# One scatter for both experts of a pair, slots turned back behind the second product, and nine load buffers

## The chip, the cores and the metric

The kernel runs on one core of one Trainium2 chip. The time is the device time of one execution, in microseconds (us). The core has TensorE for matmuls, VectorE (DVE) and ScalarE (ACT) for element by element work, GpSimd (POOL, hardly used here) and SyncE (SP), whose queue issues the loads. Each engine runs its instructions in the order in which they were laid down when the program was built, and waits on semaphores for the others.

## The reference, cut to what matters

The program is a two-layer hybrid transformer block on 256 tokens (and 256 context tokens in the first layer) of width 1024. Only the last part matters here, the mixture of experts of the second layer:

```python
def swiglu(h, w1, w3, w2):
    return (jax.nn.silu(h @ w1) * (h @ w3)) @ w2

def moe_swiglu(h, w_router, w1, w3, w2):
    logits = jnp.einsum('bnd,de->bne', h, w_router).astype(jnp.float32)
    top_vals, top_idx = lax.top_k(logits, TOP_K)          # 2 of 8 experts
    gates = jax.nn.softmax(top_vals, axis=-1)
    combine = jnp.einsum('bnk,bnke->bne', gates, jax.nn.one_hot(top_idx, N_EXPERTS, dtype=jnp.float32))
    out = jnp.zeros_like(h)
    for e in range(N_EXPERTS):
        out = out + combine[..., e:e + 1].astype(h.dtype) * swiglu(h, w1[e], w3[e], w2[e])
    return out
...
        x_lat = x_lat + mod_lat[5] * y
```

All is fp32. `w1` and `w3` are 1024 x 3584 for each expert, `w2` 3584 x 1024.

## The kernel before, in words

Experts are sorted by the number of their tokens and taken in pairs: the even expert of a pair has up to 128 slots, the odd one up to 64. A token is brought to its slot by a product with a one-hot matrix (`hot`, L1331), and the expert's rows go back by a product with the one-hots turned (`pT`).

An expert's inner width of 3584 is cut into 7 blocks of 512. `seq` (L172) gives the order of the blocks: those of a pair's two experts take turns (the first pair starts with two blocks of the even one). For each block, `experts` (L1428) does the first product with `w1` and `w3` (`hidden`, into the banks `p1` and `p3`), then the second product of the block before with `w2` (`finish`, into two banks `py` that gather all 7 blocks), so the second product runs one block late. `turn` puts the hidden values through SiLU and transposes them; TensorE's transposes stand inside the next block's first product, and ScalarE and VectorE then make `g` (odd expert) or `gh` and `gl` (even expert), which the second product needs.

Weights come in loads of 1 MiB (`load`, L106) into `raw` buffers that are used in a ring: 4 + 1 + 5 = 10. An fp32 product is done as two or three products of rounded parts, so ScalarE casts each load (`whi`, L76) and VectorE subtracts (`wlo`, L77), here called the cast and the split. There are four buffers of such pairs. A load may start when the split ten places back is done. A block takes six loads.

Once a pair, in the fourth block of the even expert, `slots_back` (L1381) transposes the pair's one-hots, copies them to `pT` (ScalarE), multiplies them with the gates and copies the result to `gs` (VectorE): the gate of each slot. One block later `one_hots` overwrites `hot` for the next pair. When an expert's 7 blocks are done, `rows` (L1515) scales its result by the gates and rounds it in two parts, `yh` (ScalarE) and `yl` (VectorE). In the next block `scatter` (L1524) multiplies them with `pT`, between the products with `w1` and `w3`, and `residual` (L406) adds eight pieces of 128 x 256 to the tokens `xl` on VectorE (L409). So each expert of a pair has its own scatter, except in the last pair, where `scatter_last` takes both. A second pass over all experts stands behind a branch and does not run here.

The order on each engine is laid down by a scheduler, which starts from the order of the code; `tc.issue_after` holds an instruction back behind another. The names in the rows: `whi`, `wlo` the parts of weights, `p` the first product, `py` the second, `pt` transposes, `pg` gates or gathered tokens, `po` the scatter's product, `u`, `g`, `sl`, `gl` steps of `turn` and of the hidden values, `xf`, `xs` gathered tokens.

Of the kernel before, what the change touches and what calls it, by code (L numbers as in the profile page):

```python
# [20 lines left out]
P = 128  # L21
# [9 lines left out]
EPS = 1e-6  # L31
RAW, RAW0, RAWF, RAW2, RAW3, WS, WS2 = 4, 5, 3, 5, 1, 3, 4
TURN = (3, 5)
# [14 lines left out]
def program(ctx, tc, a, out, upto=99, tap=None):  # L48
# [6 lines left out]
    def pool(name, bufs=1, **kw):  # L55
        return tc.tile_pool(name=name, bufs=bufs, **kw)
# [11 lines left out]
    def bank(name="ps"):  # L68
        return ps.tile([P, 512], F32, tag="ps", name=name)
# [32 lines left out]
    def buffers(*pools):  # L102

        ring[:] = [p for p, n in pools for _ in range(n)]
# [72 lines left out]
    def small_(e):  # L177
        return e % 2 == 1
# [1082 lines left out]
    wsp_st.close()  # L1261
    if RAW3:
        raw3 = ctx.enter_context(pool("raw3", RAW3, reuse_waits="tile"))
        buffers((rawp, RAW), (raw3, RAW3), (raw2, RAW2))
    wsw = ctx.enter_context(pool("wsw", WS2, reuse_waits="tile"))
# [114 lines left out]

    def slots_back(p2):  # L1381
        pt = bank("pt")
        for i in range(4):
            TE.transpose(pt[:, P * i:P * (i + 1)], hot[:, i % 2, i // 2].bitcast(F32), ident)
        S.copy(pT, pt.rearrange("p (e t) -> p e t", e=2))
        pg = bank("pg")
        for e in range(2):
            for tt in range(2):
                TE.matmul(pg[:, e:e + 1], hot[:, tt, e].bitcast(F32), gate[:, tt, 2 * p2 + e:2 * p2 + e + 1],
                          start=tt == 0, stop=tt == 1)  # L1390
        V.tensor_copy(gs[:, 2 * p2:2 * p2 + 2], pg[:, 0:2])
# [36 lines left out]
    def experts(x0, then=None):  # L1428
# [86 lines left out]
        def rows(e):  # L1515
            ys = []
            for n in range(2):
                yh, yl = (t512(f"y{z}").bitcast(F32R) for z in "hl")
                S.mul(yh, py[e][n], gs[:, e:e + 1])
                V.scalar_tensor_tensor(yl, py[e][n], gs[:, e:e + 1], yh.bitcast(F32), op0=ALU.mult, op1=ALU.subtract)  # L1520
                ys.append((yh, yl))
            return ys

        def scatter(e, ys):  # L1524
            for d2 in range(KT // 2):
                po = bank("po")
                for z, dt in enumerate((2 * d2, 2 * d2 + 1)):
                    yh, yl = ys[dt // 4]
                    c = slice(P * (dt % 4), P * (dt % 4 + 1))
                    o = po[:, NC * z:NC * (z + 1)]  # L1530
                    TE.matmul(o, yh[:, c], pT[:, e % 2], start=z == 0, stop=False, skip_group_check=True)
                    TE.matmul(o, yl[:, c], pT[:, e % 2], start=False, stop=z == 1, skip_group_check=True)
                for z in range(2):
                    residual(1, 5, 2 * d2 + z, po[:, NC * z:NC * (z + 1)], None, (1,))
# [19 lines left out]
        xg[0] = x0  # L1554
        prev = done = None
        for i, (e, f) in enumerate(seq):
# [6 lines left out]
            if i == 2 and not ids:  # L1563
                for j in range(1, EXP):
                    k = HP * (j % 2) + j // 2
                    ids[j] = nc.values_load(ords[0:1, k:k + 1].bitcast(I32), engines=[mybir.EngineType.SP],
                                            min_val=0, max_val=EXP - 1)
            if done:
                scatter(*done)
                done = None  # L1570
            hidden(p3, e)
# [18 lines left out]
            if i:  # L1590
                finish(i - 1)
                if seq[i - 1][1] == NF - 1:
                    done = seq[i - 1][0], rows(seq[i - 1][0])
            if f == 3 and e % 2 == 0:
                slots_back(e // 2)
            if f == 4 and e < EXP - 2:
                one_hots(e + 2)
        m = finish(len(seq) - 1)
        scatter_last((done, (EXP - 1, rows(EXP - 1))), m)

# [104 lines left out]
```

## Time and profile before

| | |
|---|---|
| time, median of 3 runs | 1754.49 us (1753.9 to 1755.68) |
| the profiled execution | 1755.12 us |
| its span, first to last instruction | 1752.5 us |
| TensorE busy over the span | 1666.5 us (95%) |
| VectorE busy over the span | 1464.7 us (84%) |
| ScalarE busy over the span | 1061.3 us (61%) |
| mixture-of-experts stage | about 848 to 1746 us of the span |
| loads of its weights | 335 of 1 MiB, two halves of a last one |

Times in the rows count from the span's start. Matmuls are pipelined and their ends are modelled, so a busy TensorE is not one at its peak: the distance of the starts tells its pace. Where an instruction waited, the row ends with the idle time of its engine and who ended it.

### The profile page before, as it was taken

The page shows a single profiled execution, that of the slowest core. Times are in us where ns is not written, and L with a number is a line of the kernel's source. Part 1 is how long each engine was busy: PE and PEld are TensorE (multiplying, and loading weights), DVE is VectorE, ACT ScalarE, POOL GpSimd, SP SyncE. Part 2 cuts the span into 40 slices and gives each one's busy share as a digit, 9 for nine tenths or more (in the row PEclk, how much of TensorE's full clock was granted, in tenths as well). Part 3 has the DMA queues.
Part 4 walks back from the last instruction along what each step waited for, and adds up shares of the span by engine and source line. Part 5 has one row for each costly group of instructions (what it writes and reads, how often), then busy time and mean ns, then how long its engine had stood idle before and what let it go on. Part 6 is the DMA issues. An engine that isn't in the chain of part 4 may idle for free.

```text
span 1752.5 us, 23262 instructions
## 1 busy us (share of the span) xinstructions
PE 1666.5 (95%) x8672; PEld 1389.6 (79%) x8672; DVE 1464.7 (84%) x2081; ACT 1061.3 (61%) x1145; POOL 7.4 (0%) x10
## 2 busy tenths in 40 slices
PE   6999999999999999996999989999999999999996
PEld 4777878888888999996877867778877788777885
DVE  5567599978544888886889999999999999999996
ACT  3354342222222455554788878878887788888884
POOL 0000000000000000000000000000000000000000
PEclk9999999999999999997999999999999999999998
DMA  8542554665312121254799999999989999899991
GB/s 363 203 168 107 231 216 168 263 235 198 121 48 96 66 93 66 70 213 144 291 384 386 416 342 343 409 400 412 416 327 389 404 400 419 332 378 420 399 418 65
DMA packets 65930, 474.08 MB, mean 271 GB/s; under 512 B 7312, under 2 KB 7696, under 8 KB 8464
## 3 DMA queue, kind: packets, MB, share of 16 engines
q1 hardware_dynamic: 65376, 471.79, 69.0%
q8 instruction: 70, 1.15, 0.3%
q10 hardware_dynamic: 432, 0.72, 0.1%
q14 instruction: 52, 0.43, 0.1%
HBM read 471.43 MB, written 1.05 MB: 270 GB/s over the span
## 4 chain that ended last, share of the span: by engine, by line
PE 79%; DVE 12%; issue 6%; ACT 2%; DMA 1%; DVEq 0%; SPq 0%; ACTq 0%
PE p L1445 9%; PE py L1511 7%; DVE wlo L77 7%; PE py L1507 5%; PE p L81 5%; PE p L82 5%; PE p L80 5%; PE p L1455 4%; PE p L1456 4%; PE p L1454 4%; PE po L80 3%; PE po L81 3%; PE po L82 3%; PE pp L950 2%; PE pp L949 2%
## 5 line engine op out<-in xcount | busy, mean ns | idle before, releaser
L76 ACT CAST whi<-raw 128x2048 fp32r<-128x2048 f32 (+1 forms) x458 | 760.8, 1683 | 387.1 <-PE p L81 157.4
L77 DVE TENSOR_TENSOR wlo<-raw,whi 128x2048 fp32r<-128x2048 f32 (+1 forms) x458 | 903.0, 2000 | 102.1 <-ACT whi L76 98.4
L1445 PE MATMUL p<-wlo,xs 128*128 128x512 f32 x448 | 176.6, 394 | 8.3 <-DVE wlo L77 8.3
L1445 PE MATMUL p<-whi,xs 128*128 128x512 f32 x448 | 177.8, 397 | 2.4 <-DVE xl L409 2.3
L1455 PE MATMUL p<-wlo,xh 128*128 128x512 f32 x448 | 176.0, 393 | 2.3 <-DVE wlo L77 2.3
L1454 PE MATMUL p<-whi,xh 128*128 128x512 f32 x448 | 177.8, 397 | 0.0
L1456 PE MATMUL p<-whi,xl 128*128 128x512 f32 x448 | 175.8, 392 | 0.0
L81 PE MATMUL p<-hlo,whi 128*128 128x512 f32 (+1 forms) x368 | 139.7, 381 | 0.2
L82 PE MATMUL p<-hhi,wlo 128*128 128x512 f32 (+1 forms) x368 | 139.3, 380 | 0.0
L80 PE MATMUL p<-hhi,whi 128*128 128x512 f32 (+1 forms) x368 | 138.3, 381 | 1.1 <-ACT hhi L372 1.1
L1507 PE MATMUL py<-whi,g 128*128 128x512 f32 x224 | 95.8, 430 | 18.4 <-DVE g L77 18.2
L1445 PEld LDWEIGHTS p<-wlo,xs 128*128 128x128 f32 x448 | 84.2, 188 | 29.7 <-DVE wlo L77 12.9
L1455 PEld LDWEIGHTS p<-wlo,xh 128*128 128x128 f32 x448 | 85.1, 190 | 19.4 <-DVE wlo L77 2.6
L1445 PEld LDWEIGHTS p<-whi,xs 128*128 128x128 f32 x448 | 84.2, 188 | 19.3 <-issue 2.5
L1456 PEld LDWEIGHTS p<-whi,xl 128*128 128x128 f32 x448 | 84.8, 189 | 17.8
L1454 PEld LDWEIGHTS p<-whi,xh 128*128 128x128 f32 x448 | 84.9, 189 | 16.7
L1507 PE MATMUL py<-wlo,g 128*128 128x512 f32 x224 | 93.7, 421 | 0.0
L1511 PE MATMUL py<-wlo,gh 128*128 128x512 f32 x224 | 86.6, 401 | 6.1 <-DVE wlo L77 6.1
L1511 PE MATMUL py<-whi,gl 128*128 128x512 f32 x224 | 87.1, 403 | 0.0
L950 PE MATMUL pp<-wlo,hhi 128*128 128x256 f32 x288 | 81.8, 284 | 1.2 <-DVE wlo L77 1.2
L949 PE MATMUL pp<-whi,hhi 128*128 128x256 f32 x288 | 82.5, 287 | 0.0
L1511 PE MATMUL py<-whi,gh 128*128 128x512 f32 x224 | 82.0, 395 | 0.0
(375 smaller groups left out, 3082.8 us busy)
## 6 DMA issues: line engine op xcount, KB each, us to landing
raw<-moe_w SPq DMA_DIRECT2D x335, 1024.0 KB, 8.2
raw<-ffn SPq DMA_DIRECT2D x33, 1024.0 KB, 4.8
raw<-w_mod SPq DMA_DIRECT2D x24, 1024.0 KB, 7.0
raw<-w_mod_t SPq DMA_DIRECT2D x24, 1024.0 KB, 4.8
raw<-w_in_odd SPq DMA_DIRECT2D x12, 1024.0 KB, 4.7
raw<-w_in_even SPq DMA_DIRECT2D x6, 1024.0 KB, 6.6
raw<-w_out_even SPq DMA_DIRECT2D x4, 1024.0 KB, 7.1
raw<-w_out_odd SPq DMA_DIRECT2D x4, 1024.0 KB, 4.7
```

What stands on the lines that cost most here:

```text
L76: h = S.copy(hi, full)
L77: return h, (eng or V).tensor_tensor(lo, full, hi.bitcast(F32), op=ALU.subtract)
L80: TE.matmul(o, wh, xh, start=first, stop=False, **kw)
L81: TE.matmul(o, wh, xl, start=False, stop=False, **kw)
L82: TE.matmul(o, wl, xh, start=False, stop=last, **kw)
L949: TE.matmul(po, hhi[:, kt, tk], wh[:, c], start=f, stop=False, **kw)
L1445: m = TE.matmul(po, x_, z[:, w], start=kt == 0 and z is wh, stop=kt == KT - 1 and z is wl, skip_group_check=True)
L1454: TE.matmul(po, xh[:, kt], wh[:, w], start=kt == 0, stop=False)
L1455: TE.matmul(po, xh[:, kt], wl[:, w], start=False, stop=False)
L1456: m = TE.matmul(po, xl[:, kt], wh[:, w], start=False, stop=kt == KT - 1)
L1507: m = TE.matmul(py[e][n], gT[:, ft].rearrange("p u s -> p (u s)"), w[:, 512 * n:512 * (n + 1)], start=first and w is wh, stop=last and w i ...
L1511: m = TE.matmul(py[e][n], gT[g][:, ft], w[:, 512 * n:512 * (n + 1)], start=first and g == "h" and w is wh, stop=last and g == "l")
```

## The change

`slots_back` takes the last matmul of the second product (`m`, from `finish`) and puts its transposes and gate matmuls behind it. `rows` gives the even expert tiles of its own (`ep`), so that they can wait; `done` collects both experts of a pair, and one `scatter` adds their four products in the same bank and updates the tokens once: 8 updates a pair instead of 16. For the memory the one-buffer pool `raw3` goes: nine loads in the ring.

```diff
--- before.py
+++ after.py
@@ -29,7 +29,7 @@
 EDIM = 3584
 NF = EDIM // 512
 EPS = 1e-6
-RAW, RAW0, RAWF, RAW2, RAW3, WS, WS2 = 4, 5, 3, 5, 1, 3, 4
+RAW, RAW0, RAWF, RAW2, WS, WS2 = 4, 5, 3, 5, 3, 4
 TURN = (3, 5)
 FK = 7
 KY = (2, 6)
@@ -1259,9 +1259,7 @@
 
 
     wsp_st.close()
-    if RAW3:
-        raw3 = ctx.enter_context(pool("raw3", RAW3, reuse_waits="tile"))
-        buffers((rawp, RAW), (raw3, RAW3), (raw2, RAW2))
+    buffers((rawp, RAW), (raw2, RAW2))
     wsw = ctx.enter_context(pool("wsw", WS2, reuse_waits="tile"))
     pairs[:] = [wsw] * WS2
     W.ahead = 2 * WS2 - 2
@@ -1378,16 +1376,17 @@
 
     gs = mo.tile([P, 2 * EXP], F32, name="gs")[:, :EXP]
 
-    def slots_back(p2):
+    def slots_back(p2, m):
         pt = bank("pt")
-        for i in range(4):
-            TE.transpose(pt[:, P * i:P * (i + 1)], hot[:, i % 2, i // 2].bitcast(F32), ident)
+        pg = bank("pg")
+        with tc.issue_after(m.ins):
+            for i in range(4):
+                TE.transpose(pt[:, P * i:P * (i + 1)], hot[:, i % 2, i // 2].bitcast(F32), ident)
+            for e in range(2):
+                for tt in range(2):
+                    TE.matmul(pg[:, e:e + 1], hot[:, tt, e].bitcast(F32), gate[:, tt, 2 * p2 + e:2 * p2 + e + 1],
+                              start=tt == 0, stop=tt == 1)
         S.copy(pT, pt.rearrange("p (e t) -> p e t", e=2))
-        pg = bank("pg")
-        for e in range(2):
-            for tt in range(2):
-                TE.matmul(pg[:, e:e + 1], hot[:, tt, e].bitcast(F32), gate[:, tt, 2 * p2 + e:2 * p2 + e + 1],
-                          start=tt == 0, stop=tt == 1)
         V.tensor_copy(gs[:, 2 * p2:2 * p2 + 2], pg[:, 0:2])
 
     ep = ctx.enter_context(pool("exp"))
@@ -1515,21 +1514,25 @@
         def rows(e):
             ys = []
             for n in range(2):
-                yh, yl = (t512(f"y{z}").bitcast(F32R) for z in "hl")
+                if small_(e):
+                    yh, yl = (t512(f"y{z}").bitcast(F32R) for z in "hl")
+                else:
+
+                    yh, yl = (ep.tile([P, 512], F32R, tag=f"y{z}{n}", name=f"y{z}") for z in "hl")
                 S.mul(yh, py[e][n], gs[:, e:e + 1])
                 V.scalar_tensor_tensor(yl, py[e][n], gs[:, e:e + 1], yh.bitcast(F32), op0=ALU.mult, op1=ALU.subtract)
                 ys.append((yh, yl))
             return ys
 
-        def scatter(e, ys):
+        def scatter(both):
             for d2 in range(KT // 2):
                 po = bank("po")
-                for z, dt in enumerate((2 * d2, 2 * d2 + 1)):
-                    yh, yl = ys[dt // 4]
-                    c = slice(P * (dt % 4), P * (dt % 4 + 1))
-                    o = po[:, NC * z:NC * (z + 1)]
-                    TE.matmul(o, yh[:, c], pT[:, e % 2], start=z == 0, stop=False, skip_group_check=True)
-                    TE.matmul(o, yl[:, c], pT[:, e % 2], start=False, stop=z == 1, skip_group_check=True)
+                for j, (e, ys) in enumerate(both):
+                    for z, dt in enumerate((2 * d2, 2 * d2 + 1)):
+                        c = slice(P * (dt % 4), P * (dt % 4 + 1))
+                        for k, y in enumerate(ys[dt // 4]):
+                            TE.matmul(po[:, NC * z:NC * (z + 1)], y[:, c], pT[:, e % 2], start=j == z == k == 0,
+                                      stop=j == z == k == 1, skip_group_check=True)
                 for z in range(2):
                     residual(1, 5, 2 * d2 + z, po[:, NC * z:NC * (z + 1)], None, (1,))
 
@@ -1552,7 +1555,7 @@
                             out[:, NC * (dt - 1):NC * (dt + 1)], xs[1][:, dt - 1:dt + 1].rearrange("p k t -> p (k t)"))
 
         xg[0] = x0
-        prev = done = None
+        prev, done = None, []
         for i, (e, f) in enumerate(seq):
             p1, p3 = bank("p1"), bank("p3")
             hidden(p1, e, None if prev is None else lambda m: turn(i - 1, prev, m))
@@ -1565,9 +1568,9 @@
                     k = HP * (j % 2) + j // 2
                     ids[j] = nc.values_load(ords[0:1, k:k + 1].bitcast(I32), engines=[mybir.EngineType.SP],
                                             min_val=0, max_val=EXP - 1)
-            if done:
-                scatter(*done)
-                done = None
+            if len(done) == 2:
+                scatter(done)
+                done = []
             hidden(p3, e)
             if small_(e):
                 prev = [t512("c") for _ in range(2)]
@@ -1588,15 +1591,15 @@
             if i == len(seq) - 1:
                 turn(i, prev)
             if i:
-                finish(i - 1)
+                m = finish(i - 1)
                 if seq[i - 1][1] == NF - 1:
-                    done = seq[i - 1][0], rows(seq[i - 1][0])
+                    done.append((seq[i - 1][0], rows(seq[i - 1][0])))
             if f == 3 and e % 2 == 0:
-                slots_back(e // 2)
+                slots_back(e // 2, m)
             if f == 4 and e < EXP - 2:
                 one_hots(e + 2)
         m = finish(len(seq) - 1)
-        scatter_last((done, (EXP - 1, rows(EXP - 1))), m)
+        scatter_last((*done, (EXP - 1, rows(EXP - 1))), m)
 
     experts(gather(0, True), gates)
     most = nc.values_load(most_i[0:1, 0:1], min_val=0, max_val=NC)
```

The order of the instructions as it was laid down, at three places, all on VectorE. First, pair 1 around `slots_back`, in the seventh block of the pair. Before:

```order
L1474 TENSOR_TENSOR u<-pt,u 128x256 x2
L77 TENSOR_TENSOR wlo<-raw,whi 128x2048
L1476 TENSOR_TENSOR u<-u 128x256
L1391 COPY gs<-pg 128x2
L1338 TENSOR_SCALAR hot<-const 128x128 x3
L77 TENSOR_TENSOR wlo<-raw,whi 128x2048
L77 TENSOR_TENSOR g<-u,g 128x4x64
L1338 TENSOR_SCALAR hot<-const 128x128
L77 TENSOR_TENSOR wlo<-raw,whi 128x2048
L1581 TENSOR_TENSOR sl<-sl,p_10268 128x512
L77 TENSOR_TENSOR wlo<-raw,whi 128x2048 x4
```

After the change:

```order
L1473 TENSOR_TENSOR u<-pt,u 128x256 x2
L77 TENSOR_TENSOR wlo<-raw,whi 128x2048
L1475 TENSOR_TENSOR u<-u 128x256
L77 TENSOR_TENSOR wlo<-raw,whi 128x2048
L77 TENSOR_TENSOR g<-u,g 128x4x64
L77 TENSOR_TENSOR wlo<-raw,whi 128x2048
L1584 TENSOR_TENSOR sl<-sl,p_10253 128x512
L77 TENSOR_TENSOR wlo<-raw,whi 128x2048
L1336 TENSOR_SCALAR hot<-const 128x128
L1390 COPY gs<-pg 128x2
L1336 TENSOR_SCALAR hot<-const 128x128 x3
L77 TENSOR_TENSOR wlo<-raw,whi 128x2048 x3
```

The copy to gs and the one-hots moved from ahead of g to behind sl and a third split. On TensorE the four transposes and the gate matmuls moved from ahead of the sixteen matmuls py<-g to behind them. The first pair had this order before, too.

Second, the end of pair 1, where the next pair's first blocks have begun. In both fences u and g belong to the odd expert's last block, and yl is the odd expert's, whose second product needs g. Before:

```order
L1474 TENSOR_TENSOR u<-pt,u 128x256 x2
L77 TENSOR_TENSOR wlo<-raw,whi 128x2048
L1476 TENSOR_TENSOR u<-u 128x256
L409 SCALAR_TENSOR_TENSOR xl<-po,mods_91,xl 128x256 x2
L77 TENSOR_TENSOR g<-u,g 128x4x64
L409 SCALAR_TENSOR_TENSOR xl<-po,mods_91,xl 128x256 x6
L77 TENSOR_TENSOR wlo<-raw,whi 128x2048 x2
L1581 TENSOR_TENSOR sl<-sl,p_11317 128x512
L77 TENSOR_TENSOR wlo<-raw,whi 128x2048 x2
L1520 SCALAR_TENSOR_TENSOR yl<-py,gs,yh 128x512 x2
L77 TENSOR_TENSOR wlo<-raw,whi 128x2048 x2
L1493 TENSOR_TENSOR gl<-pt,gh 128x512
```

After the change:

```order
L1473 TENSOR_TENSOR u<-pt,u 128x256 x2
L77 TENSOR_TENSOR wlo<-raw,whi 128x2048
L1475 TENSOR_TENSOR u<-u 128x256
L77 TENSOR_TENSOR wlo<-raw,whi 128x2048
L77 TENSOR_TENSOR g<-u,g 128x4x64
L77 TENSOR_TENSOR wlo<-raw,whi 128x2048
L1584 TENSOR_TENSOR sl<-sl,p_11302 128x512
L77 TENSOR_TENSOR wlo<-raw,whi 128x2048
L1523 SCALAR_TENSOR_TENSOR yl<-py,gs,yh 128x512
L77 TENSOR_TENSOR wlo<-raw,whi 128x2048
L1523 SCALAR_TENSOR_TENSOR yl<-py,gs,yh 128x512
L409 SCALAR_TENSOR_TENSOR xl<-po,mods_91,xl 128x256
```

The even expert's eight updates (xl) are gone from both sides of g, and g stands behind two splits here where one stood (four and three, counted from the last xf). Behind these rows come, before, the odd expert's eight updates in a row; after the change, a split, two updates, a split, gl and five updates, each for both experts.

Third, pair 0, where the even expert ends two blocks ahead of the odd one; the place is behind the even expert's second yl. Before:

```order
L77 TENSOR_TENSOR wlo<-raw,whi 128x2048
L409 SCALAR_TENSOR_TENSOR xl<-po,mods_91,xl 128x256 x2
L77 TENSOR_TENSOR wlo<-raw,whi 128x2048
L409 SCALAR_TENSOR_TENSOR xl<-po,mods_91,xl 128x256 x2
L77 TENSOR_TENSOR wlo<-raw,whi 128x2048
L1474 TENSOR_TENSOR u<-pt,u 128x256 x2
L409 SCALAR_TENSOR_TENSOR xl<-po,mods_91,xl 128x256
L1476 TENSOR_TENSOR u<-u 128x256
L409 SCALAR_TENSOR_TENSOR xl<-po,mods_91,xl 128x256 x2
L77 TENSOR_TENSOR g<-u,g 128x4x64
L409 SCALAR_TENSOR_TENSOR xl<-po,mods_91,xl 128x256
L77 TENSOR_TENSOR wlo<-raw,whi 128x2048 x6
```

After the change:

```order
L77 TENSOR_TENSOR wlo<-raw,whi 128x2048 x3
L1473 TENSOR_TENSOR u<-pt,u 128x256 x2
L77 TENSOR_TENSOR wlo<-raw,whi 128x2048
L1475 TENSOR_TENSOR u<-u 128x256
L77 TENSOR_TENSOR wlo<-raw,whi 128x2048
L77 TENSOR_TENSOR g<-u,g 128x4x64
L77 TENSOR_TENSOR wlo<-raw,whi 128x2048 x4
```

The eight updates are gone, and five splits instead of three stand ahead of g.

## Rows read from the trace of the kernel before

**Rows 1.** Busy us by window: total, PE, PEld, DVE, ACT, POOL, clock, DMA share, GB/s
```profile
848.00:1746.00 898.00, 857.58 (x4009) 701.35 (x4007) 845.25 (x623) 723.43 (x609) 0.00 (x0) 0.98 0.94 373
...
1110.00:1160.00 50.00, 49.92 (x229) 40.35 (x228) 49.77 (x31) 43.21 (x35) 0.00 (x0) 1.00 1.01 420
```

**Rows 2.** Chain of waits, 1100 to 1300: start us, us, what
```profile
1105.35 3.94 PE py L1507 x16
...
1134.61 3.92 PE py L1507 x16
...
1168.41 5.43 PE py L1507 x16
...
1198.78 3.63 PE py L1507 x16
...
1256.52 1.75 PE pg L1411 x16
```

**Rows 3.** Table of waits, 800 to 1753: total us, times, longest
```profile
DVE gs L1391 <- PE pg L1389: 11.3, 3, 3.8
...
DVE wlo L77 <- DMA raw<-moe_w: 1.4, 1, 1.4
```

**Rows 4.** Timeline of VectorE, 1150 to 1175: start, us, instruction [idle before <-releaser]
```profile
1165.07 0.16 DVE L1391 COPY gs<-pg 128x2 f32<-128x2 f32 x1 [3.78 <-PE pg L1389]
```

**Rows 5.** Timeline of TensorE, same place
```profile
1163.65 0.60 PE L1384 MATMUL pt<-const,hot 128*128 128x128 f32 x4
1164.09 0.95 PE L1389 MATMUL pg<-const,hot 128*128 128x1 f32 x8
1168.41 0.79 PE L1507 MATMUL py<-whi,g 128*128 128x512 f32 x1 [3.37 <-DVE g L77]
```

**Rows 6.** Timeline of VectorE, end of pair 1
```profile
1293.35 0.41 DVE L77 TENSOR_TENSOR g<-u,g 128x256 fp32r<-128x256 f32 x1
1293.68 2.44 DVE L409 SCALAR_TENSOR_TENSOR xl<-po,mods,xl 128x256 f32<-128x256 f32 x6
```

**Rows 7.** Timeline of ScalarE, end of pair 1
```profile
1299.61 0.69 ACT L1519 ACTIVATE yh<-py,gs 128x512 fp32r<-128x512 f32 x1 [1.59 <-PE py L1507]
```

**Rows 8.** Timeline of TensorE, end of pair 1
```profile
1287.70 0.28 PE L1531 MATMUL po<-pT,yh 128*128 128x256 f32 x1
...
1290.41 0.40 PE L1454 MATMUL p<-whi,xh 128*128 128x512 f32 x1
...
1317.23 0.50 PE L1511 MATMUL py<-wlo,gh 128*128 128x512 f32 x1 [2.09 <-DVE wlo L77]
```

**Rows 9.** Timeline of VectorE, pair 0
```profile
1025.58 0.88 DVE L409 SCALAR_TENSOR_TENSOR xl<-po,mods,xl 128x256 f32<-128x256 f32 x2 [0.47 <-PE po L1532]
...
1033.73 0.41 DVE L77 TENSOR_TENSOR g<-u,g 128x256 fp32r<-128x256 f32 x1
...
1034.46 13.29 DVE L77 TENSOR_TENSOR wlo<-raw,whi 128x2048 fp32r<-128x2048 f32 x6
...
1053.63 0.42 DVE L77 TENSOR_TENSOR g<-u,g 128x256 fp32r<-128x256 f32 x1
```

**Rows 10.** Timeline of TensorE, pair 0
```profile
1029.59 0.47 PE L1445 MATMUL p<-whi,xs 128*128 128x512 f32 x1 [2.33 <-DVE xl L409]
```

**Rows 11.** Busy us by window, columns as in rows 1: the clock
```profile
1168.30:1171.70 3.40, 3.29 (x8) 2.61 (x9) 3.40 (x5) 0.17 (x1) 0.00 (x0) 0.50 0.85 294
1029.59:1033.00 3.41, 3.41 (x15) 2.83 (x16) 3.41 (x6) 0.42 (x1) 0.00 (x0) 1.00 1.04 341
```

**Rows 12.** Timeline of TensorE, the end
```profile
1733.67 0.79 PE L1507 MATMUL py<-whi,g 128*128 128x512 f32 x1 [4.99 <-DVE g L77]
```

**Rows 13.** Timeline of VectorE, the end
```profile
1741.35 0.75 DVE L1520 SCALAR_TENSOR_TENSOR yl<-py,gs,yh 128x512 fp32r<-128x512 f32 x1 [0.54 <-ACT yh L1519]
```

**Rows 14.** Instructions on raw, 860 to 1740: ns min/median/max, landing us
```profile
L76 ACT CAST whi<-raw x324: 1889/1914/1954, 858.7 to 1727.6; 128x2048 fp32r<-128x2048 f32 x162
...
DMA to landing us min/median/max: 4.9/8.3/11.0
```

## The prediction

> **What bounds the kernel now.** I read the busy times by window first, then the chain of work that ended last, then the table of who waited for whom, and last the timeline of each engine where the change works. The change touches only the mixture-of-experts stage, from about 848 to 1746 us of the span. There VectorE is busy 845.25 of 898.00 us and TensorE 857.58; in a quiet window of 50 us they stand at 49.77 and 49.92, and the transfers at a share of 1.01 and 420 GB/s [rows 1]. So three resources are nearly full, and the reader is to see in the chain which of them sets the pace. From the second product of one odd expert to the next it took 1134.61 - 1105.35 = 29.26 us [rows 2], which I call a cycle (twelve loads of 1 MiB). TensorE could do it faster: 120 large matmuls at 3.63/16 = 0.227 us [rows 2] are 27.2 us, and 12 transposes come on top. VectorE sets it: a split (wlo) takes (13.29 - 0.09)/6 = 2.20 us from start to start [rows 9], twelve of them 26.4, and small operations fill the rest. The cycle from 1134.61 to 1168.41 took 33.80 us, 4.5 more: the one with slots_back.
>
> So time is gained where VectorE stands idle or has less to do, not where TensorE has less. In the table of waits one idle time of VectorE belongs to the slots alone: gs <- PE pg, 11.3 us in 3 times [rows 3].
>
> **The change part by part.** The sum is made against the profiled execution, 1755.12 us (span 1752.5); the median of the runs shown is 0.63 lower.
>
> *Slots behind the second product.* The copy into gs waited 3.78 us [rows 4]; three one-hots, a split and g stood behind it on VectorE, and the second product needs g. gs waited for the gate matmuls, which stood on TensorE behind the whole first product, at 1164.09; then TensorE sat 3.37 us for g [rows 5]. VectorE waited for TensorE for something nobody needed soon, and TensorE for VectorE. In the new order two splits and sl stand between g and the first one-hot, with gs behind it, and TensorE's small instructions stand behind the sixteen matmuls of the second product. Those take 3.63 us [rows 2] and the small ones 1.2 to 1.4 [rows 5], so they end about 5 us after g; VectorE reaches the one-hot 2 x 2.20 and sl, also 5 to 5.5 us after g. The cover is 0.3 us or so, and I take 3.5 of the 3.78 us. The copies and one-hots themselves remain. ScalarE's pT cast goes behind three casts; what is queued behind it are casts for splits two ahead. The first pair has gs behind the second product already, so the gain comes three times: 3 x 3.5 = -10.5 us. Bounds: -11.3 (the whole wait) and 0 (it only moves). Late next is VectorE's own work, so TensorE's smaller gap and the slow clock behind it give nothing beyond this.
>
> *One scatter per pair.* TensorE's matmuls stay the same in number. VectorE loses 8 of 16 updates (xl) a pair, in three pairs, at 2.44/6 = 0.40 us [rows 6]: 9.6 us if VectorE's work alone counts. I don't take that, because at these places the order shows a loop through TensorE.
>
> Ends of the two middle pairs. Before, g stood behind three splits and two xl, now behind four splits: 2.2 - 0.8 = 1.4 us later than 1293.35 [rows 6]. TensorE no longer has the even expert's scatter there (1290.41 - 1287.70 = 2.7 us [rows 8]); it arrives that much earlier, waits about 2 us, and starts the second product 0.5 us earlier than before. VectorE has one split more done by then, and is 2.9 us ahead, six xl and a split's start counted. Then ScalarE's yh, which waits for that product [rows 7], stands in front of the cast of the second split after it, which costs VectorE some 0.8 us. Left are -2.1 us at the split that TensorE waited for at 1317.23 [rows 8]. If TensorE runs the product behind its wait at the lower clock, 16 matmuls take 5.43 instead of 3.63 us [rows 2], yh comes 1.8 later, and -0.3 is left. The rows decide this neither way: after the wait of 3.37 us the granted clock was 0.50 (1.2 GHz) in 1168.30 to 1171.70, after one of 2.33 us it was 1.00 (2.4 GHz) in 1029.59 to 1033.00 [rows 5, 10, 11]. I take the middle, -1.3 each, -2.6 for both; ends 0 and -3.2 each.
>
> Pair 0. Its even expert ends two blocks ahead of the odd one, and its xl lay between three splits ahead of g. Now g stands behind five splits: 4.4 us more, less seven xl (2.8) and VectorE's wait of 0.47 in front of them, so 1.1 later than 1033.73 [rows 9]. TensorE, without that scatter and its wait of 2.33 us [rows 10], is there some 5 us earlier, and waits about 6 us in one piece. Behind it come 48 large matmuls (10.9 us), 8 transposes (under 1 us) and a gather of 32 (2 x 1.75 [rows 2]), some 15.3 in all, and then one operation, a split and the next g on VectorE. That g starts at about 1035.2 + 15.3 + 2.6 = 1053.1 against 1053.63 before [rows 9], and with 1.8 us of slow matmuls at 1054.9. After a wait that long I expect slow matmuls for the most part: +0.8; ends +1.5 and -3.7 (VectorE's whole saving). The doubled scatter at this pair's end, 16 small matmuls more, I cost at nothing: TensorE waits for splits behind it, and VectorE's order there is that of before; without this cover it is 2 us.
>
> The rule that speaks against the change is in the Trainium skill, "TensorE: Matmul & The Clock Gate", section "HAM oscillation": gaps without matmuls between bursts send the array back to half clock, and the burst behind the gap pays. The rows just named show both outcomes. Were it so behind each of these waits, the sum would be -10.5 - 0.6 + 1.3 + 0.7 = -9.1; behind none, -10.5 - 4.2 - 0.5 + 0.7 = -14.5.
>
> *The end.* Even rows now have tiles of their own, so the last even expert's first yl stands ahead of VectorE's part of the last g: 0.7 us [rows 13]. TensorE waits there already, 4.99 us [rows 12], and waits longer: +0.7. The yl had idle time behind g before, so nothing comes back. Bounds 0 and +1.5 (both yl).
>
> *Nine loads.* SyncE issues a load when the split ten places back (now nine) has freed its buffer. Ten buffers at 29.26/12 = 2.44 us are 24.4 us, nine 22.0. Of this a cast and a split take 1.91 + 2.2, and the landing 8.3 at the median, 11.0 at most [rows 9, 14]: 6.9 us are left in the worst case. In the table VectorE waited for a load once, 1.4 us [rows 3]. I take 0; 0 to +14.5 are the ends, the latter under the fourth rival.
>
> Sum: -10.5 - 2.6 + 0.8 + 0.7 = -11.6, so 1743.5 for a run like the profiled one and 1742.9 beside the median: I forecast 1743. Its own range, by the clock, is 1740 to 1746.
>
> **Rivals.**
> 1. *VectorE's work is all that counts.* Then its wait and its removed updates come back in full: 11.3 + 9.6 - 0.7 = 20.2, so 1734. For it: 49.77 of 50 us busy in a quiet window. Against: at the ends of pairs the order puts g, yl and xl behind results of TensorE.
> 2. *The ends of pairs cost.* Pair 0 brings +1.5, the two others nothing, the end +1.5, and a late one-hot takes 0.5 of each gain with the slots: -9.0 + 3.0 = -6.0, so 1748.5. For it: g moves behind more splits, and TensorE's waits fall together into one. Against: VectorE is ahead by those splits afterwards.
> 3. *The wait only moves.* The first one-hot overwrites what the transposes read, with 0.3 us of cover; if the second product starts late, one-hots and gs wait as long as before, and with the other terms all is about 1753. Against: the first pair has gs in this place, and no wait for it is in the table (3 times, not 4).
> 4. *Nine buffers starve the splits: slower.* At 420 GB/s [rows 1] a load takes 2.50 us, a cycle 29.95, 0.69 more than VectorE's 29.26. Today the lead of the loads shrinks by that in each cycle and is made up while slots_back and the pair's end wait; the change takes this pause and one buffer away. If the lead is gone, transfers set 21 cycles: +14.5, and with the -11.6 it ends at +2.9, 1757.5. It decides from the point where the shrinking, some 4 us in six cycles, eats the 6.9 us left; by these rows it does not reach that.
>
> **How the numbers follow.** Forecast 0.62, rivals 0.15, 0.12, 0.06 and 0.05. 0.2% of the time is 3.5 us, about what a measurement of this kernel can tell from no change. Faster (under 1751): 0.62 + 0.15 + 0.12 = 0.89; within it, the third, 0.06; slower, the fourth, 0.05. The range takes in the forecast's own, the first rival and the second: 1734 to 1749.
>
> **What would show it.** Right: no wait of gs for pg over 0.5 us; second products of odd experts 29.3 us apart, and 33.80 - 3.5 = 30.3 in the cycle with slots; 24 updates fewer; one wait of TensorE of about 6 us in pair 0 near 1029, and of about 2 us at the next two ends of pairs; no cast or split waiting for a load. Wrong: waits for raw in the steady cycles, one-hots or gs waiting over 2 us, or low clock at more places than before.

## The result and the profile after

The changed kernel took 1740.24 us (median of 4, 1733.17 to 1741.93) where the kernel before took 1755.09 (1753.9 to 1758.1) beside it: a ratio of 0.9898, 95% interval 0.9885 to 0.9911, or -14.9 us. Forecast were -11.6 us and 1743.

The profiled execution is the fastest of the four, 1733.17 us, and it flatters. Its second product of the first odd block starts at 899.93 us of the span, before it 905.16: 5.23 us are gained where, of the change, only the ring of nine loads can have acted, and the kernel with nine loads alone stands at 906.46 there. The same kernel run again stood at 904.67 and took 1739.25. So I read distances from that product on. From there to the last odd second product before took 828.51 us, after 813.27: -15.24.

The page of the changed kernel, busy us: VectorE has 24 instructions fewer (the updates), TensorE's work is the same but for the clock.

```profile
span 1731.4 us, 23231 instructions
PE 1658.6 (96%) x8672; PEld 1384.0 (80%) x8672; DVE 1453.9 (84%) x2057; ACT 1061.9 (61%) x1145; POOL 7.4 (0%) x10
```

**The slots.** VectorE's timeline at the place of [rows 4] (start, us, instruction, idle before):

```profile
1156.73 0.42 DVE L1475 TENSOR_TENSOR u<-u 128x256 f32<-128x256 f32 x1
1157.07 2.29 DVE L77 TENSOR_TENSOR wlo<-raw,whi 128x2048 fp32r<-128x2048 f32 x1
1159.27 0.42 DVE L77 TENSOR_TENSOR g<-u,g 128x256 fp32r<-128x256 f32 x1
1159.92 2.29 DVE L77 TENSOR_TENSOR wlo<-raw,whi 128x2048 fp32r<-128x2048 f32 x1 [0.23 <-ACT whi L76]
1162.13 0.68 DVE L1584 TENSOR_TENSOR sl<-sl,p 128x512 f32<-128x512 f32 x1
1162.73 2.29 DVE L77 TENSOR_TENSOR wlo<-raw,whi 128x2048 fp32r<-128x2048 f32 x1
1164.93 0.28 DVE L1336 TENSOR_SCALAR hot<-const 128x128 fp32r<-128x128 f32 x1
1165.13 0.15 DVE L1390 COPY gs<-pg 128x2 f32<-128x2 f32 x1
1165.20 0.67 DVE L1336 TENSOR_SCALAR hot<-const 128x128 fp32r<-128x128 f32 x3
```

TensorE at the same place, the answer to [rows 5]:

```profile
1159.75 0.50 PE L1506 MATMUL py<-whi,g 128*128 128x512 f32 x1
...
1163.52 0.60 PE L1384 MATMUL pt<-const,hot 128*128 128x128 f32 x4
1163.95 0.95 PE L1387 MATMUL pg<-const,hot 128*128 128x1 f32 x8
```

The wait of 3.78 us is gone, and so is TensorE's of 3.37. The gates are ready at 1164.9, just when VectorE comes to the one-hots. The cycle, 33.80 us in [rows 2], is now as long as the one before it (chain of waits after: start, us, what):

```profile
1101.18 3.92 PE py L1506 x16
...
1130.46 3.92 PE py L1506 x16
...
1159.75 3.93 PE py L1506 x16
...
1190.01 3.79 PE py L1506 x16
```

The cycle with slots takes 1159.75 - 1130.46 = 29.29 us, the next one 30.1. By windows (total us, busy PE, PEld, DVE, ACT, POOL, clock, DMA share, GB/s) over the two cycles, before:

```profile
1134.61:1198.62 64.01, 60.63 (x277) 49.94 (x277) 59.48 (x42) 51.83 (x42) 0.00 (x0) 0.97 0.99 401
```

and after:

```profile
1130.46:1189.88 59.42, 59.31 (x277) 48.49 (x277) 58.95 (x41) 51.81 (x42) 0.00 (x0) 1.00 1.01 419
```

VectorE's idle time falls from 64.01 - 59.48 = 4.53 us to 0.47, by 4.06, and the stretch falls by 4.59. Of this 0.55 is given back in the third cycle (28.73 before, 29.28 after), which leaves 4.04.

The next cycle of 30.1 us is not VectorE's. The last pair makes no one-hots, and its cycle behind the slots takes 30.11 us too; TensorE, with the slots' 12 small matmuls in it, is busy all the time, and so it is in the 28.75 us of the cycle after (windows, after, columns as above):

```profile
1601.22:1631.33 30.11, 30.11 (x145) 25.15 (x145) 29.58 (x20) 26.43 (x22) 0.00 (x0) 1.00 1.01 420
1631.33:1660.08 28.75, 28.75 (x134) 23.56 (x132) 28.70 (x18) 25.27 (x20) 0.00 (x0) 1.00 1.01 419
```

**The ends of pairs 1 and 2.** At both, TensorE waits the same 1.95 us for g (timeline of TensorE, after):

```profile
1287.11 0.50 PE L1506 MATMUL py<-whi,g 128*128 128x512 f32 x1 [1.95 <-DVE g L77]
...
1508.64 0.50 PE L1506 MATMUL py<-whi,g 128*128 128x512 f32 x1 [1.95 <-DVE g L77]
```

The product behind the wait ran at full clock both times. Yet the two cycles take 69.42 us at end 1 and 71.04 at end 2, since at end 2 a stretch ahead of the wait ran at half clock. TensorE had just done 32 gather matmuls, and its last stop, 0.66 us, had ended at 1482.35; end 1 has the same gather, the same short stop and no such stretch (window, after):

```profile
1488.10:1491.50 3.40, 3.40 (x9) 2.67 (x8) 3.40 (x4) 3.00 (x4) 0.00 (x0) 0.50 1.01 402
```

**Pair 0.** VectorE's g comes behind five splits (timeline of VectorE, the answer to [rows 9]):

```profile
1027.43 2.28 DVE L77 TENSOR_TENSOR wlo<-raw,whi 128x2048 fp32r<-128x2048 f32 x1
1029.63 0.42 DVE L77 TENSOR_TENSOR g<-u,g 128x256 fp32r<-128x256 f32 x1
1030.76 2.29 DVE L77 TENSOR_TENSOR wlo<-raw,whi 128x2048 fp32r<-128x2048 f32 x1 [0.71 <-ACT whi L76]
1035.57 2.29 DVE L77 TENSOR_TENSOR wlo<-raw,whi 128x2048 fp32r<-128x2048 f32 x1 [2.52 <-ACT whi L76]
```

and TensorE, the answer to [rows 10]:

```profile
1026.94 0.52 PE L1444 MATMUL p<-whi,xs 128*128 128x512 f32 x1 [1.89 <-ACT whi L76]
1029.77 0.79 PE L1444 MATMUL p<-wlo,xs 128*128 128x512 f32 x1 [2.31 <-DVE wlo L77]
1030.36 0.63 PE L1506 MATMUL py<-whi,g 128*128 128x512 f32 x1
```

It is not one wait for g but one for a cast and one for a split, and the product runs at a mean clock of 0.65 (window 1030.36 to 1035.70, after):

```profile
1030.36:1035.70 5.34, 5.34 (x17) 4.26 (x17) 2.42 (x2) 2.27 (x2) 0.00 (x0) 0.65 1.00 397
```

**The end.** The answer to [rows 12]: 5.55 us of waiting where 4.99 stood.

```profile
1713.20 0.80 PE L1506 MATMUL py<-whi,g 128*128 128x512 f32 x1 [5.55 <-DVE g L77]
```

### The profile page after: what moved, and what is told of

It is laid out like the page before. It is cut to its first block, busy times and chain, and to the rows that moved or that the text cites. A ratio compares the mean times of both kernels' runs of the same rounds, so it can differ in the third digit from the quotient of the medians.

```text
span 1731.4 us, 23231 instructions
## 1 busy us (share of the span) xinstructions
PE 1658.6 (96%) x8672; PEld 1384.0 (80%) x8672; DVE 1453.9 (84%) x2057; ACT 1061.9 (61%) x1145; POOL 7.4 (0%) x10
## 3 DMA queue, kind: packets, MB, share of 16 engines
HBM read 471.43 MB, written 1.05 MB: 273 GB/s over the span
## 4 chain that ended last, share of the span: by engine, by line
PE 74%; DVE 16%; issue 8%; ACT 2%; DMA 0%; DVEq 0%; SPq 0%; ACTq 0%
DVE wlo L77 10%; PE p L1444 9%; PE py L1506 6%; PE py L1510 5%; PE p L81 5%; PE p L82 5%; PE p L80 5%; PE po L80 4%; PE po L81 3%; PE po L82 3%; PE p L1454 3%; PE p L1453 3%; PE p L1455 3%; PE pp L950 2%; PE pp L949 2%
## 5 line engine op out<-in xcount | busy, mean ns | idle before, releaser
L1454 PEld LDWEIGHTS p<-wlo,xh 128*128 128x128 f32 x448 | 84.6, 189 | 19.2 <-DVE wlo L77 2.6
L1444 PEld LDWEIGHTS p<-whi,xs 128*128 128x128 f32 x448 | 84.5, 189 | 19.2 <-ACT whi L76 2.8
L1453 PEld LDWEIGHTS p<-whi,xh 128*128 128x128 f32 x448 | 84.5, 189 | 16.7
```

The lines of the kernel that those rows point to most:

```text
L1444: m = TE.matmul(po, x_, z[:, w], start=kt == 0 and z is wh, stop=kt == KT - 1 and z is wl, skip_group_check=True)
L1453: TE.matmul(po, xh[:, kt], wh[:, w], start=kt == 0, stop=False)
L1454: TE.matmul(po, xh[:, kt], wl[:, w], start=False, stop=False)
```

## Experiments

Distances in us, from one odd second product to a later one, in the profiled run of each kernel. *Stage* is from the first to the last of them; *slots* the three cycles with slots_back; *pair 0* the four cycles around its end; *ends* two cycles each; *last* the last cycle. The kernel before was run again beside the experiments, on three chips: its median was 1756.17 us beside the changed kernel again, the slots, the scatter and the nine loads, 1756.09 beside pair 0 apart, the end as before, two scatters late and the one-hots, and 1756.65 beside seven loads, zero matmuls and three edits. Ratios are to these; a difference between rows of two chips is only as good as they agree.

| kernel | median | stage | slots | pair 0 | end 1 | end 2 | last |
|---|---|---|---|---|---|---|---|
| before | 1755.09 | 828.51 | 100.79 | 105.66 | 72.93 | 71.88 | 23.28 |
| changed | 1740.24 | 813.27 | 87.84 | 106.71 | 69.42 | 71.04 | 23.84 |
| changed, again | 1739.43 | 813.62 | 87.83 | 107.09 | 69.41 | 72.62 | 23.84 |
| slots alone | 1743.76 | 815.66 | 87.83 | 106.44 | 71.89 | 71.91 | 23.26 |
| scatter and loads alone | 1754.05 | 825.23 | 100.76 | 106.66 | 69.42 | 71.02 | 23.78 |
| nine loads alone | 1755.89 | 828.08 | 100.71 | 107.04 | 72.90 | 71.89 | 23.26 |
| pair 0 apart | 1739.67 | 815.12 | 87.83 | 107.02 | 69.41 | 72.64 | 23.83 |
| end as before | 1738.47 | 812.95 | 87.84 | 107.11 | 69.44 | 72.61 | 23.28 |
| two scatters late | 1754.31 | 825.35 | 87.83 | 111.10 | 73.80 | 75.40 | 23.84 |
| seven loads | 1735.48 | 810.72 | 87.83 | 105.71 | 69.45 | 71.06 | 23.84 |
| one-hots on GpSimd | 1739.18 | 813.80 | 87.80 | 106.68 | 71.00 | 71.05 | 23.84 |
| zero matmuls | 1733.08 | 809.04 | 87.83 | 102.55 | 69.41 | 71.03 | 23.85 |
| three edits | 1730.88 | 805.32 | 87.84 | 103.65 | 69.42 | 69.42 | 23.29 |

**The slots alone.** The kernel before, with (cut; the gate matmuls stand inside the `with`, too)

```diff
-    def slots_back(p2):
+    def slots_back(p2, m):
...
+        with tc.issue_after(m.ins):
+            for i in range(4):
+                TE.transpose(...)
...
-                finish(i - 1)
+                m = finish(i - 1)
-                slots_back(e // 2)
+                slots_back(e // 2, m)
```

> The kernel before with one part of the change: slots_back's transposes and gate matmuls behind the second product. Two scatters a pair and ten loads stay. Theory A (each term by itself, as in the prediction): VectorE's wait for the gates, 11.3 us in three times, goes, and nothing takes its place: the distance of the odd experts' second products in the three cycles with slots falls from 33.2 to 33.8 us to about 29.3, the next cycle takes 30.1 because it holds the one-hots and gs; together -10.5 to -13 us, 1742 to 1744.5. Rival B (VectorE's work is all that counts): exactly its idle time goes, -11.3, 1743.5; A and B part only in the run with the scatter alone. Rival C (the wait only moves, and what was gained came from the scatter): gs or the one-hots wait over 2 us behind the second product, and the time is 1751 or more.

Ratio 0.9925 (0.9912 to 0.9938) to before's 1756.17: -12.4 by the medians. The table of waits has 0.3 us for gs where 11.3 stood. A and B both fit here; C is out. One detail of A is not right: 30.1 us is no sign of the one-hots, as the last pair shows above.

**The scatter and the loads alone.** The changed kernel with before's slots_back.

> The changed kernel with slots_back as before: one scatter for both experts of a pair, tiles of its own for the even expert's rows, nine loads; the transposes and gate matmuls stand ahead of the second product again. Theory A: the wait of gs for the gates is back, three times 3.8 us; of the scatter only -1 to -3 us in all are left (pair 0 about +1, the ends of pairs 1 and 2 -0.3 to -3 each by the clock behind TensorE's wait, the end +0.6), so 1752 to 1754. Rival B (VectorE's work is all that counts): the 24 updates that went are 9.6 us, less 0.7 at the end, so -8.9, 1746. A rival of the other side (the late scatter costs by itself): 1756 or more.

Ratio 0.9988 (0.9978 to 0.9998), -2.1 us. The wait is back, 3.79 us (timeline of VectorE):

```profile
1166.85 0.16 DVE L1389 COPY gs<-pg 128x2 f32<-128x2 f32 x1 [3.79 <-PE pg L1387]
```

Theory A holds. B, 24 updates of 0.40 us back in full, is out for the whole: -2.1 was measured, not -8.9. But the places differ, as the next windows show.

At end 1, with no stretch of slow clock in either, the kernel with the slots alone and the changed one differ by 2.48 us, and VectorE's work by 2.83 (two cycles, columns as above; slots alone, then changed):

```profile
1258.54:1330.43 71.89, 66.86 (x330) 54.41 (x329) 69.83 (x67) 56.88 (x55) 0.00 (x0) 1.00 0.92 350
...
1251.72:1321.13 69.41, 65.81 (x330) 54.53 (x329) 67.00 (x59) 56.85 (x55) 0.00 (x0) 1.00 0.94 360
```

So there most of the removed work came back. At pair 0 none did: VectorE's busy time in the four cycles falls from 99.58 us (slots alone) to 96.54 (changed, again), and its idle time grows from 6.86 to 10.55.

**Nine loads alone.** Before without `raw3`.

> The kernel before with nothing but the ring of loads cut from ten to nine. Theory A: nothing, 1754.5 to 1755.5 (within 0.2%), and no cast or split waits for a load more often than the one time, 1.4 us, of before. Rival D (nine buffers starve the splits): waits for raw in many cycles and up to +14.5, 1769; a gain is not expected by anyone.

Ratio 0.9998 (0.9989 to 1.0007): nothing. No wait of a cast or split for a load is in its table of waits.

**The changed kernel again**, unedited.

> The changed kernel once more, on the chip that runs its parts, to tell the size and the spread. Its profiled run of 1733.17 us stood 5.2 us ahead of the kernel before at 905 us, where no instruction is changed yet, and 21.1 at the end. If that lead is chance (the places where TensorE's clock falls differ from run to run), most runs of the changed kernel lie near 1740, with -14 to -16 against the kernel before, and the profile shows the odd experts' second products of the slots cycles 29.3 us apart, whatever the lead at 905 us is. If the lead is a lasting effect of the change, this run has it again, and most runs lie near 1734.

Ratio 0.9902 (0.9888 to 0.9917). The lead of 5 us at 905 us was chance: no other run of the table has it. This run also shows the end of pair 2 at the other clock. The same wait, and the first matmul behind it takes 0.80 us, not 0.50 as at 1508.64 above:

```profile
1512.16 0.80 PE L1506 MATMUL py<-whi,g 128*128 128x512 f32 x1 [1.95 <-DVE g L77]
```

The windows behind the two waits of this run, pair 1 and pair 2:

```profile
1290.62:1294.30 3.68, 3.68 (x16) 3.07 (x17) 3.52 (x3) 2.11 (x3) 0.00 (x0) 1.00 1.00 376
1512.16:1515.57 3.41, 3.41 (x8) 2.76 (x9) 3.25 (x3) 1.93 (x2) 0.00 (x0) 0.50 1.01 418
```

One kernel, the same code, the same wait: 2.4 GHz behind the one, 1.2 GHz behind the other, and the two cycles at the end of pair 2 take 72.62 us, where the first profile had 71.04. Both have the slow stretch ahead of the wait; in the kernel with three edits, where the granted clock stayed at 1.00 over the whole place, the two cycles take 69.42, as at end 1. One slow stretch costs 1.6 us here.

**Pair 0 apart** (the flag that ends the sum in a bank is set to fit, here and in the two scatters below).

```diff
-            if len(done) == 2:
+            if len(done) == 2 or done and done[0][0] < 2:
```

> The changed kernel, but in pair 0 each expert has its own scatter, as before. The prediction gave +0.8 us to the late scatter of this pair, so this kernel would be 0.8 faster, 1738.6. Against the run with the slots alone, which has this place in the order of before, the changed kernel takes 72.8 to 73.2 us for the three cycles behind 994 us and that one 72.7: by this the gain is 0.1 to 0.5. Rival (VectorE's work is all that counts): eight updates of 0.40 us come back, +3.2, 1742.6. Telling it apart: in the profile VectorE's idle time in these cycles (10.2 us in the changed kernel, 6.8 with the slots alone) falls by about what the updates add.

1739.67 us beside 1739.43: no difference, neither the 0.8 of the prediction nor the 3.2 of the rival, and the four cycles take 107.02 and 107.09. The late scatter of this pair neither costs nor brings anything that these runs can tell.

**The end as before.**

```diff
-                if small_(e):
+                if small_(e) or e == EXP - 2:
```

> The changed kernel, but the last even expert's rows use the shared tiles again, so its first yl stands behind the last g. The prediction gave +0.7 us to the yl ahead of g; if that holds, this kernel is 0.5 to 0.7 faster, 1738.7 to 1738.9, and the distance from the last but one odd second product to the last falls from 23.84 to about 23.3 us. Rival: the end is set by the transfers or by the clock, and the time stays within 0.2 of the changed kernel's.

The last cycle falls from 23.84 to 23.28 us, 0.56, as expected; the median, 1738.47, is 0.96 lower, but its interval (0.9875 to 0.9907) holds the changed kernel's ratio.

**Two scatters, late.** Sixteen updates again, all at the late place.

```diff
-                scatter(done)
+                for one in done:
+                    scatter([one])
```

> The changed kernel with sixteen updates a pair again in place of eight, both scatters at the late place; g and the splits keep their order. Theory A1 (at the ends of pairs VectorE has no idle time left, so the updates themselves are the price; in the trace it is idle 4.6 us in the four cycles around the end of pair 1, and 4.1 with the slots alone): +2.5 to +3.2 us for each of the three pairs, +7.5 to +9.6, 1747 to 1749. Theory A2 (what the late scatter brought is that TensorE reaches the second product earlier, and that g no longer stands behind updates): the updates lie in waiting time, and the kernel loses 3 us at most, 1742.5 or less.

1754.31 us: 14.9 above the changed kernel, much beyond both theories; 11.7 of it lie in the stage, and 2.3 were there at the first odd second product already. The three ends take 2.8 to 4.4 us more (end 1, at the same clock up to the updates, 4.4). VectorE does thirteen updates in a row at end 1 where it did five:

```profile
1313.21 5.17 DVE L409 SCALAR_TENSOR_TENSOR xl<-po,mods,xl 128x256 f32<-128x256 f32 x13
...
1330.74 2.29 DVE L77 TENSOR_TENSOR wlo<-raw,whi 128x2048 fp32r<-128x2048 f32 x1 [0.69 <-ACT whi L76]
1333.53 0.43 DVE L1475 TENSOR_TENSOR u<-u 128x256 f32<-128x256 f32 x1 [0.49 <-ACT u L1474]
```

That is 3.2 us of updates, and 1.2 of VectorE's waiting behind them. TensorE's second scatter had to wait, too, 1.24 us for an update and 2.48 for what the profile names as gl, the instruction ahead of the thirteen (timeline of TensorE):

```profile
1310.25 0.35 PE L1534 MATMUL po<-pT,yh 128*128 128x256 f32 x1 [1.24 <-DVE xl L409]
1313.44 0.36 PE L1534 MATMUL po<-pT,yh 128*128 128x256 f32 x1 [2.48 <-DVE gl L1492]
```

Behind it, from 1314.5, TensorE ran at half clock for a stretch, so how much of the 1.2 us is the wait and how much the clock is open. A1 names the right kind of price and is too low. Against the slots alone (71.89) the late place costs +1.9 with sixteen updates, and halving them brings -4.4, the slow stretch in it; the change is the sum of the two, -2.5.

**One-hots on GpSimd.**

```diff
-                one_hots(e + 2)
+                one_hots(e + 2, G)
```

> The changed kernel with the four one-hots of the next pair made on GpSimd instead of VectorE, three times (12 instructions; on VectorE they take 0.20 us each from start to start, 0.28 in the row). Theory A1 (in the steady cycles VectorE's work sets the pace): the cycle after the slots takes 29.3 instead of 30.1 us, three times, -2.4, 1737. Rival (GpSimd disturbs VectorE while it runs, or the gather of the next pair waits for it): the time stays or rises, 1739.5 or more, and a split beside it takes longer than its 2.2 us.

1739.18 us, no difference. VectorE is rid of about 0.77 us, the time from its first one-hot to the next split less the copy to gs, but the cycle behind the slots still takes 30.10; only the one after that falls, from 29.28 to 28.82. Theory A1 fails. By its windows TensorE is the bound there: in the last pair, which has no one-hots in any of these kernels, the two cycles take 30.1 and 28.75 as well. The shortest cycles in any of these profiles, 28.73 to 28.82, are then its own pace, and the transposes and gate matmuls add 1.2 to 1.4 [rows 5]. A kernel with less work for TensorE was not tried. If this reading holds, the steady cycle sits only half a microsecond above a second floor.

**Zero matmuls in TensorE's waits**, with the added function and one of the four places:

```diff
+    def fill(o, n):
+        for _ in range(n):
+            TE.matmul(o, zero, tm["h"][:, 0, 0:512], start=False, stop=False, skip_group_check=True)
...
+            with tc.issue_after(m.ins) if i == len(seq) - 1 else ExitStack():
+                fill(py[e][0], FILL.get(i, 0))
```

> The changed kernel with 64 additional matmuls of a zero weight (they add nothing to the result) on TensorE where it waits: 28 in pair 0 in front of the last splits of the odd expert's sixth block and of the next block, 8 at each end of pairs 1 and 2, 20 ahead of the last second product. No other engine's order changes. In the run of the changed kernel these waits are 2.0, 2.6, 2.6, 2.1, 2.1 and 5.7 us, and 18 to 23 us in this neighbourhood run at half clock (0.50). Theory C (the waits let the clock fall, and the slow products behind them are on the path): the second products behind the waits run at full clock, 16 in 3.6 instead of 5.4 to 5.9 us, and pair 0, the end of pair 2 and the end give back 1.5 to 2 us each, 1732.5 to 1735. Theory E (VectorE's pace hides TensorE's slow stretches): the clock rises and the time stays, 1739 to 1740. Rival: the added matmuls stand in the way, 1741 or more.

1733.08 us, ratio 0.9864 (0.9848 to 0.9881): 6.3 below the changed kernel run again, on another chip. Theory C holds, though not at every place: end 1 takes what it took, and ahead of end 2's wait a stretch from 1491.1 was slow all the same. At the end (timeline of TensorE) the added matmuls fill 4.75 us, and what is left to wait is 0.97:

```profile
1710.68 4.75 PE L1383 MATMUL py<-tmh,zero 128*128 128x512 f32 x20
1716.39 0.50 PE L1519 MATMUL py<-whi,g 128*128 128x512 f32 x1 [0.97 <-DVE g L77]
```

The second products behind the filled waits (pair 0 twice, the end) run at full clock, sixteen in 3.6 us:

```profile
1037.70:1041.30 3.60, 3.60 (x17) 3.00 (x16) 2.29 (x1) 2.14 (x2) 0.00 (x0) 1.00 0.95 385
1055.44:1059.10 3.66, 3.66 (x17) 3.04 (x17) 2.99 (x4) 2.55 (x3) 0.00 (x0) 1.00 0.95 360
...
1716.39:1720.00 3.61, 3.60 (x16) 3.00 (x17) 0.00 (x0) 0.04 (x1) 0.00 (x0) 1.00 0.00 0
```

Pair 0 gives back 4.5 us, more than the 1.5 to 2 expected; the end of pair 2 is 1.6 shorter than in the run again, but the first of the two profiles of the changed kernel had 71.04 without the fill. From the last odd second product to the end of the span it takes 16.6 us instead of 19.2 (18.2 in the first profile of the changed kernel).

**Seven loads in the ring** (`RAW2` 3 instead of 5).

> The changed kernel with seven loads in the ring instead of nine (the buffers of an earlier stage's prefetch shrink with it, from five to three). By the reserve of the prediction seven buffers of 2.44 us are 17.1 us; a cast and a split take 4.1, the longest landing 11.0, and 2.0 us are left: no starving, 1739 to 1741. Rival D (the lead of the loads shrinks by 0.69 us a cycle, some 4 us in six cycles): 2.0 us are not enough, casts wait for raw in the steady cycles, and the time goes up by as much as 14.5, to 1745 to 1754.

1735.48 us: nothing starves. Casts now wait for loads, but shortly and on ScalarE, which has time (table of waits: total us, times, longest):

```profile
ACT whi L76 <- DMA raw<-moe_w: 8.8, 19, 0.6
```

That it came out 4 us lower than the changed kernel was expected by nobody; the intervals of the two ratios, 0.9862 to 0.9895 here and 0.9888 to 0.9917 there, overlap. In its profile the shorter places are pair 0 and end 2, where fewer stretches ran at half clock; whether the ring has a part in that, or an order that changed by a few instructions with it, was not tried and stays open.

**Three edits together**: the end as before, the one-hots on GpSimd, the zero matmuls.

> The changed kernel with three edits at once: the last even expert's rows in the shared tiles (measured alone: the last cycle 0.56 us shorter), the one-hots of the next pair on GpSimd (alone: 28.82 instead of 29.28 us in the second cycle after the slots, 0.46 three times, the median not measurably different), and the 64 zero matmuls in TensorE's waits. By the first two alone -1.9, 1737.5; with theory C of the zero matmuls -6 to -8, 1731.5 to 1733.5; with theory E 1737.5.

1730.88 us, ratio 0.9854 (0.9837 to 0.9870), -25.8 by the medians: the best of all, 9.4 below the median of the changed kernel's first runs.

## Why the prediction was right, and where it was not

*What bounds the kernel.* Right: VectorE's order sets the pace, and time came from its idle time. It missed how near a second floor lies. It put TensorE's own pace at 27.2 us and twelve transposes; the cycles in which TensorE never stops take 28.73 to 28.82, against 29.28.

*Slots, forecast -10.5.* The mechanism was right; the size was off. Alone it is -12.4 by the medians; in the two profiles the lead grows by 4.0, 5.0 and 4.1 us over the three places. I took 3.5 of 3.78 us because the cover seemed only 0.3. It was enough, and 0.3 more of short waits went too (4.53 - 0.47 = 4.06 of idle time). The second place had a stretch of slow clock before, at 1393.6, and gave 5. The forecast cycle was wrong in a detail: 30.3 us was to be the cycle with slots; it takes 29.3, and the next one 30.1, which is TensorE's time with the slots' matmuls in it.

*Ends of pairs 1 and 2, forecast -1.3 each, a middle of -2.1 and -0.3 by the clock.* The middle was taken as one cost and is really a count of slow stretches (and of -2.1 and -0.3 it is -1.2, not -1.3). Measured against the slots alone, at full clock an end gives -2.5: end 1 in both profiles of the changed kernel, end 2 in the kernel with three edits. Each slow stretch takes 1.6 back: end 2 had one in the first profile, -0.9, and two in the second, +0.7. Together the ends gave -3.4 and -1.8, and that the forecast of -2.6 lies between is luck with the clock. The wait of about 2 us was 1.95. The Trainium skill ("TensorE: Matmul & The Clock Gate", section "HAM oscillation") tells how gaps send the array back to half clock; its example has longer gaps. Here half clock came behind one wait of 1.95 us and not behind the other, and at end 2 also where the last stop, of 0.66 us, lay 5.8 us back, so counting waits does not give the slow stretches.

*Pair 0, forecast +0.8.* g came 1.1 us later by the order, as forecast: 1029.63, or 1034.86 with the 5.23 added, against 1033.73 [rows 9]. The step that failed is the single wait of 6 us for g: TensorE stopped first for a cast and a split, since every split ahead of g feeds a matmul ahead of it too. And the +1.05 of the first pair of profiles is not the change: before's profiled run was quick here (105.66, in the kernel with nine loads alone 107.04). By the experiment it is 0. The work saved there went into VectorE's idle time. The clock has a part in that, too: its mean over the four cycles is 0.97 with the slots alone and 0.92 in the changed kernel, and with zero matmuls in the waits the cycles take 102.55 us. These runs do not tell the two apart.

*The end, forecast +0.7.* 0.56.

*Nine loads, forecast 0.* Right, and seven would do.

*The rivals.* That VectorE's work is all that counts fell as a sum with the scatter alone, 2.1 us instead of 8.9. It does hold at ends 1 and 2 as long as the clock stays up: 2.5 of 2.8 us of work came back. What makes 24 updates worth 2 us is that the eight of pair 0 brought nothing, that the slow stretches at end 2 took 1.6 or 3.2 us, and that the end cost 0.56. Where updates stand in a row at the late place they cost their full time and more (4.4 us for eight, a slow stretch in it). The second, third and fourth rivals did not come.

Together: -12.4 and -2.1 are -14.5, against -14.9 for all and -16.7 in the second set of runs; the parts add up within what the clock's places make of a run. By the differences the forecast, -11.6, was 3.3 us short, 1.9 of it from the slots and 1.0 from the rest.

## What to carry to other kernels

A wait of the busiest engine for something that nobody needs soon was worth its full length here, and the few tenths of waiting behind it as well; count the engine's idle time over the cycles before and after, and the difference is the gain. Work taken off the busiest engine is worth what its place makes it: at pair 0 nothing, at the other ends 2.5 of 2.8 us, in a row at a full place more than its own time. Where TensorE waits and the product behind it is on the path, matmuls that add zero can be worth more than the next reordering; here they took 6.3 us, the end's reordering about 0.6, the whole planned change 14.9.

## What the runs showed of the hardware

- The granted clock is not fixed by the code: of two equal waits of 1.95 us one was followed by 1.00, the other by 0.50. The clock also fell 5.8 us behind a stop of only 0.66 us, with 32 gather matmuls between, and did not at the same place of the pair before. Runs of one kernel differ by such places, at least in part: 1733.17 to 1741.93 us for the changed kernel, and a lead of 5.23 us at 905 us that the next run of it did not have (some 2 us of it were there by 47 us of the span).
- With matmuls of a zero weight in waits of 2 to 5.7 us, the products behind these waits ran at 1.00; VectorE's and ScalarE's busy time stayed at 1455 and 1062 us (1454 and 1062 in the changed kernel). With the three edits together two stretches in pair 0 (from 1022.9 and from 1050.2) ran at 0.50 all the same, and the four cycles took 103.65 us, not 102.55.
- A one-hot of 128x128 takes 0.28 us on VectorE and 2.57 at the median on GpSimd (1.09 to 4.52) while VectorE is busy, and the three splits beside it took 6.88 us instead of 6.69 (timeline of VectorE, one-hots on GpSimd):

```profile
1171.05 6.88 DVE L77 TENSOR_TENSOR wlo<-raw,whi 128x2048 fp32r<-128x2048 f32 x3
```
